# Token-stationary projections behind the first attention input, their transposes, and LayerNorm sums kept in PSUM

## Chip, core and metric

The kernel runs on one core of a Trainium2 chip. The metric is device time of one execution in microseconds. A core has a matrix engine (PE, whose weight loads are a row of their own, PEld), a vector engine (DVE), a scalar engine (ACT), a general engine (POOL) and a queue engine (SP) that issues most transfers. PE writes only to PSUM, which has eight banks of 512 fp32 columns on 128 partitions. Each engine works through its own instructions in program order; semaphores tie the engines to each other and, where the builder asks for it, an engine to its own earlier instructions.

## The reference

Two layers on `x` of 256 tokens by 2048 channels, fp32. Layer one is dilated attention with a gate, layer two a Conformer convolution module with a gate. What matters here:

```python
x = x + mixer_a(rmsnorm(x, g0)) # 3 x 16 heads, ends in  y @ a_w_out   (2048 x 2048)
h = rmsnorm(x, g1)
proj = h @ b_w_in + b_in        # 2048 x 6144
a, ga, z = split(proj, 3)
u = a * sigmoid(ga)
u = causal_depthwise_conv(u, conv_w, width=31) + conv_b
u = (u - mean(u)) * rsqrt(var(u) + EPS) * ln_g + ln_b      # over the 2048 channels
x = x + (silu(u) * silu(z)) @ b_w_out + b_out
```

## The kernel before

Every fp32 product is made of three products of reduced-precision parts: weights `hi` and `lo`, tokens `h` and `l`, in the order hi·h, hi·l, lo·h. Weights come in 480 chunks of 128 x 1024, numbered `n`: 320 for the first input projection (`w_in`), 32 for `w_out`, 96 for the second mixer's input (`v_in`), 32 for `v_out`. The text counts the chunks of `v_in` as k = 0 to 95. `stage(n + 3)` loads chunk n + 3 and has ACT cast `hi`; `low_engine` picks DVE or POOL for `lo` = raw - hi. There are five buffers of each, so a cast for chunk n + 3 needs PE to be done with chunk n - 2.

The main loop runs over n: stage, then the products of chunk n on PE, then the small functions that `at(n, fn)` has put behind that chunk, then `run_line`. Nothing reorders instructions later: what is written first stands first on its engine.

- The first projection (`project`) holds 128 tokens still and moves 512 weight columns: 12 products a chunk.
- All later projections (`project_out`, `products`, `project_b`) hold 128 weight columns still and move 256 tokens: 24 products a chunk, with the result transposed, channels on partitions.
- The convolution is a DVE line (`conv_line`): for each of 16 channel tiles j, `conv_first` has ACT write two accumulators `c[0]` and `c[1]`, `conv_tap` adds 29 taps in turn to one and the other, and `conv_merge` joins them into `d[:, j]`. `run_line` takes from this line as much as its costs (0.4 us a tap) allow per chunk, so the line fills DVE while PE goes through `v_in`. The accumulators lie in two PSUM banks: tags `s` and `o` for even j, two `t` banks for odd j.
- For LayerNorm POOL sums `d` (`usum`, `dsum`) and its squares (`qsum`) in SBUF. After channel 6 a provisional mean `mu` is taken off. `ln_sums` sums over partitions by small products with `ones` on PE, `ln_spread` spreads the scale and the shift over the partitions, and five functions `norm` to `norm_low` per channel pair then make the operands of `v_out`.
- RMS statistics of the second layer (`r1_sums`, `r1_spread`) take a sum over partitions and a spread on PE as well.

Of the kernel before, what the change touches and what calls it, by code (L numbers as in the profile page):

```python
# [17 lines left out]
P = 128  # L18
# [23 lines left out]
def hybrid_kernel(ctx: ExitStack, tc: tile.TileContext, x_perm, x_tok, x_nat, vecs, rel, onehot, maskrow,  # L42
                  w_in, w_out, v_in, v_out, out):
# [31 lines left out]
    units, z_next = [], 0  # L75
    for j in range(KT):
        units += [2 * j, 2 * j + 1]
        if j % 2 and j > 2:
            units.append(32 + z_next)
            z_next += 1  # L80
    units += [32 + j for j in range(z_next, KT)]
# [432 lines left out]

    def project_out(n, n0, mh, ml, tag):

        hi, lo = staged.pop(n)
        m = n - n0
        if m < KT:
            if m == 0:  # L520
                oacc["w"] = [acc_tile(f"{tag}w{i}") for i in range(4)]
            for ct in range(8):
                acc = oacc["w"][ct // 2][:, (ct % 2) * S:(ct % 2 + 1) * S]
                wh, wl = hi[:, ct * P:(ct + 1) * P], lo[:, ct * P:(ct + 1) * P]

                nc.tensor.matmul(acc, lhsT=wh, rhs=mh[:, m, :], start=m == 0 and ct % 2 == 0, stop=False,  # L526
                                 skip_group_check=True)
                nc.tensor.matmul(acc, lhsT=wh, rhs=ml[:, m, :], start=False, stop=False, skip_group_check=True)  # L528
                nc.tensor.matmul(acc, lhsT=wl, rhs=mh[:, m, :], start=False, stop=m == KT - 1, skip_group_check=True)  # L529
                oacc[ct] = acc  # L530
        else:
            ct, half = 8 + (m - KT) // 2, m % 2
            if half == 0:
                oacc[ct] = acc_tile(f"{tag}{ct}")[:, :S]
            products(oacc[ct], hi, lo, half, mh, ml)
# [42 lines left out]
    def h_split(ct):
        g1 = vec[:, V_G1 + ct:V_G1 + ct + 1]
        nc.scalar.activation(f.hh[:, ct, :], f.x1[:, ct, :], AF.Copy, scale=g1)  # L580
        nc.vector.scalar_tensor_tensor(f.hl[:, ct, :], f.x1[:, ct, :], g1, f.hh[:, ct, :].bitcast(F32),
                                       op0=ALU.mult, op1=ALU.subtract)

    at(N_A, load_residual)
    at(N_A + 14, open_second)
    for ct in range(KT):
        if ct < 8:
            at(N_A + KT - 1, residual, ct)
            at(N_A + KT + ct // 2, h_split, ct)
            at(N_A + KT + ct // 2, square_sum, ct)  # L590
        else:
            e = N_A + KT + 2 * (ct - 8) + 1
            at(e, residual, ct)
            at(e, h_split, ct)
            at(e, square_sum, ct)
# [7 lines left out]
    def r1_sums():  # L603
        f.ps = acc_tile("ps_r1")
        token_sums(f.ps, 0, f.ss1)
        st = f.pool.tile([P, 2], F32, name="st_r1")
        nc.vector.tensor_copy(st, f.ps[:, :2])
        f.rc = f.pool.tile([P, 2], F32, name="rc_r1")
        rsqrt_mean(f.rc, st, D, 2)

    def r1_spread():
        spread(f.ps, S, f.rc)
        nc.scalar.copy(f.r1, f.ps[:, S:2 * S])

    at(N_WO, r1_sums)
    at(N_WO + 1, r1_spread)


    acc_b = {}

    def project_b(n):
        hi, lo = staged.pop(n)
        i, half = divmod(n - N_WO, 2)
        if half == 0:
            acc_b[units[i]] = acc_tile(f"b{units[i]}")[:, :S]
        products(acc_b[units[i]], hi, lo, half, f.hh, f.hl)
# [3 lines left out]
    HALF_J = 6  # L630
    clock = [0.0]
# [4 lines left out]
    def run_line(now):  # L636
        clock[0] = max(clock[0], now)
        while line and clock[0] < now + 2.64:
            cost, fn, args = line.pop(0)[1:]
            fn(*args)  # L640
            busy(cost)


    def glu_gate(j):
        f.tg = f.pool.tile([P, S], F32, tag="tg", name=f"tg{j}", bufs=2)
        nc.vector.tensor_tensor(f.tg, acc_b.pop(2 * j + 1), f.r1, op=ALU.mult)
        bg = V_BIN + 16 + j
        nc.scalar.activation(f.tg, f.tg, AF.Sigmoid, bias=vec[:, bg:bg + 1])
        busy(0.34)

    def glu_value(j):
        f.ta = acc_b.pop(2 * j)
        nc.vector.tensor_tensor(f.ta, f.ta, f.r1, op=ALU.mult)
        busy(0.34)

    def glu(j):
        u = f.pool.tile([P, TAPS - 1 + S], F32, tag="u", name=f"u{j}", bufs=3)
        nc.gpsimd.memset(u[:, :TAPS - 1], 0.0)
        nc.vector.scalar_tensor_tensor(u[:, TAPS - 1:], f.ta, vec[:, V_BIN + j:V_BIN + j + 1], f.tg,
                                       op0=ALU.add, op1=ALU.mult)  # L660
        busy(0.4)
        if j == 0:
            conv_line(j, u)
        else:
            at(f.n + 1, conv_line, j, u)
# [25 lines left out]
    def conv_merge(j, c):  # L691
# [6 lines left out]
        if j == 0:  # L698
            nc.gpsimd.tensor_copy(f.usum, f.d[:, 0, :])
        elif j < HALF_J:  # L700
            nc.gpsimd.tensor_tensor(f.usum, f.usum, f.d[:, j, :], op=ALU.add)
            if j == HALF_J - 1:
                at(f.n + 2, mid_sums)
                at(f.n + 4, mid_spread)
        elif j == HALF_J:
# [3 lines left out]
            at(f.n + 1, gather, 0)  # L709
            at(f.n + 2, gather, j)  # L710
            for i in range(1, j):
                at(f.n + 2 + 4 * i, gather, i)
        else:
            gather(j)
            if j == KT - 1:
                at(f.n + 1, ln_sums)

    def mid_sums():

        f.ps = acc_tile("ps_mid")  # L720
        token_sums(f.ps, 0, f.usum)
        f.mc = f.pool.tile([P, 2], F32, name="mc")
        nc.vector.tensor_scalar(f.mc, f.ps[:, :2], 1.0 / (HALF_J * P), None, op0=ALU.mult)

    def mid_spread():
        spread(f.ps, S, f.mc)
        nc.scalar.copy(f.mu, f.ps[:, S:2 * S])

    def gather(j):
        d = f.d[:, j, :]  # L730
        eng = nc.vector if j == KT - 1 else nc.gpsimd
        if j == 0:
            nc.scalar.activation(f.qsum, d, AF.Square)
# [3 lines left out]
        eng.tensor_tensor(f.qsum, f.qsum, sq, op=ALU.add)  # L737

        if j == HALF_J:
            nc.gpsimd.tensor_copy(f.dsum, d)  # L740
        elif j > HALF_J:
            eng.tensor_tensor(f.dsum, f.dsum, d, op=ALU.add)

    def ln_sums():
        f.ps = acc_tile("ps_ln")
        token_sums(f.ps, 0, f.dsum)
        token_sums(f.ps, 2, f.qsum)
# [197 lines left out]
```

## Time and profile before

| what | value |
|---|---|
| median of 3 runs | 1452.47 us (1452.23 to 1452.49) |
| profiled execution, its own time | 1452.36 us |
| its span, first to last instruction | 1450.6 us |
| PE busy | 1442.3 us, 99% |
| DVE busy | 960.2 us, 66% |
| ACT busy | 727.0 us, 50% |
| POOL busy | 423.7 us, 29% |
| `v_in` stage | 1074.1 to 1355.1 us of the span |
| `v_out` stage | 1355.2 to 1447.4 us of the span |
| granted TensorE clock | 1.000 |

The profiled time is 1.8 us over its span and agrees with the median to 0.1 us. Busy time of DVE, ACT and PE counts an instruction from its start to its end; the next one may start before that end, so a pitch (start to start) can be shorter than a duration.

### The profile page before, as it was taken

What the parts mean: (1) busy time and instruction counts of PE and PEld (TensorE: products, weight loads), DVE (VectorE), ACT (ScalarE), POOL (GpSimd) and SP (SyncE); (2) the same over time, 40 slices, a digit from 0 to 9 for tenths busy, and PEclk for the clock granted to TensorE, in tenths of its full rate; (3) what the DMA queues carried; (4) which work ended last, traced back from release to release, by engine and by line L of the source; (5) the groups of instructions that cost most, each with busy time, mean ns of one, the idle gap of its engine ahead of it and who ended that gap; (6) DMA issues with size and microseconds to landing.
All of it is one profiled execution on the core that took longest, in us unless ns stands there. A gap on an engine that the chain in (4) does not pass through costs nothing.

```text
span 1450.6 us, 22407 instructions
## 1 busy us (share of the span) xinstructions
PE 1442.3 (99%) x8524; PEld 1275.6 (88%) x8524; DVE 960.2 (66%) x1542; ACT 727.0 (50%) x1027; POOL 423.7 (29%) x339
## 2 busy tenths in 40 slices
PE   9999999999999999999999999999999999999999
PEld 7778888888888888888888888889999999999999
DVE  6656765765676576576567657646758989997621
ACT  7445554454455455445445545444545545555632
POOL 0210020011011002001001100207217979998544
PEclk9999999999999999999999999999999999999999
DMA  9458556557556655755755665566564655555544
GB/s 360 139 202 251 161 185 206 173 164 217 170 164 197 194 165 181 207 170 170 216 169 164 197 193 165 180 189 218 163 197 165 204 162 182 192 180 184 184 158 142
DMA packets 108699, 271.28 MB, mean 187 GB/s; under 512 B 42416, under 2 KB 44720, under 8 KB 108592
## 3 DMA queue, kind: packets, MB, share of 16 engines
q1 hardware_dynamic: 108160, 269.58, 58.2%
q8 instruction: 67, 1.10, 0.3%
q14 instruction: 40, 0.33, 0.1%
q10 hardware_dynamic: 432, 0.28, 0.1%
HBM read 267.46 MB, written 2.36 MB: 186 GB/s over the span
## 4 chain that ended last, share of the span: by engine, by line
PE 98%; DMA 1%; DVE 0%; ACT 0%; issue 0%; SPq 0%; POOL 0%; POOLq 0%; ACTq 0%
PE acc L290 60%; PE b L541 6%; PE b L542 6%; PE b L543 6%; PE psq L327 1%; PE wow L526 1%; PE vo L543 1%; PE vo L542 1%; PE vo L541 1%; PE vow L529 1%; PE vow L528 1%; PE vow L526 1%; PE wo L543 1%; PE wo L541 1%; PE wo L542 1%; PE wow L528 1%
## 5 line engine op out<-in xcount | busy, mean ns | idle before, releaser
L114 ACT CAST hi<-raw 128x1024 fp32r<-128x1024 f32 x479 | 497.0, 1048 | 292.7 <-PE acc L290 164.2
L117 DVE TENSOR_TENSOR lo<-raw,hi 128x1024 fp32r<-128x1024 f32 x358 | 441.3, 1234 | 282.2 <-ACT hi L114 275.7
L290 PE MATMUL acc<-hi,xh 128*128 128x512 f32 x1280 | 506.0, 397 | 0.1
L290 PE MATMUL acc<-lo,xh 128*128 128x512 f32 x1280 | 497.4, 391 | 0.8 <-DVE lo L117 0.8
L290 PE MATMUL acc<-hi,xl 128*128 128x512 f32 x1280 | 495.9, 389 | 0.0
L117 POOL TENSOR_TENSOR lo<-raw,hi 128x1024 fp32r<-128x1024 f32 x121 | 294.0, 2453 | 120.4 <-ACT hi L114 101.6
L290 PEld LDWEIGHTS acc<-lo,xh 128*128 128x128 f32 x1280 | 240.1, 188 | 53.4 <-DVE lo L117 1.2
L290 PEld LDWEIGHTS acc<-hi,xh 128*128 128x128 f32 x1280 | 240.5, 188 | 49.0 <-issue 2.0
L290 PEld LDWEIGHTS acc<-hi,xl 128*128 128x128 f32 x1280 | 240.8, 188 | 47.1 <-DVE xl L152 0.2
L129 POOL TENSOR_SCALAR rq<-ss 128x4 f32<-128x4 f32 x48 | 10.9, 226 | 789.7 <-DVE ss L309 787.8
L541 PE MATMUL b<-hh,hi 128*128 128x256 f32 x768 | 217.8, 284 | 0.0
L542 PE MATMUL b<-hl,hi 128*128 128x256 f32 x768 | 217.3, 283 | 0.0
L543 PE MATMUL b<-hh,lo 128*128 128x256 f32 x768 | 217.3, 283 | 0.0
L688 DVE SCALAR_TENSOR_TENSOR c<-u,vec,c 128x256 f32<-128x256 f32 x464 | 187.4, 481 | 3.5 <-ACT c L684 3.5
L542 PEld LDWEIGHTS b<-hl,hi 128*128 128x128 f32 x768 | 147.4, 192 | 0.0
L541 PEld LDWEIGHTS b<-hh,hi 128*128 128x128 f32 x768 | 147.4, 192 | 0.0
L543 PEld LDWEIGHTS b<-hh,lo 128*128 128x128 f32 x768 | 147.4, 192 | 0.0
L403 ACT ACTIVATE pr<-sc,m 128x512 f32<-128x512 f32 x32 | 23.1, 723 | 100.8 <-DVE m L401 100.8
L340 DVE TENSOR_TENSOR qk<-psq,qk 128x256 fp32r<-128x256 f32 x48 | 20.3, 422 | 50.6 <-ACT qk L339 50.6
L338 ACT CAST qk<-psq 128x256 fp32r<-128x256 f32 x48 | 17.9, 372 | 64.1 <-PE psq L327 63.6
L130 POOL TENSOR_TENSOR rq<-rq,nhalf 128x4 f32<-128x4 f32 x48 | 48.4, 1008 | 4.0
L422 ACT CAST pp<-pt 128x512 fp32r<-128x512 f32 x32 | 18.8, 587 | 44.1 <-PE pt L414 42.8
(167 smaller groups left out, 1668.0 us busy)
## 6 DMA issues: line engine op xcount, KB each, us to landing
raw<-w_in SPq DMA_DIRECT2D x319, 512.0 KB, 4.2
raw<-v_in SPq DMA_DIRECT2D x96, 512.0 KB, 3.3
raw<-w_out SPq DMA_DIRECT2D x32, 512.0 KB, 4.2
raw<-v_out SPq DMA_DIRECT2D x32, 512.0 KB, 4.1
bt<-btab SPq DMA_DIRECT2D x64, 128.0 KB, 5.8
x_tok<-x_tok SPq DMA_DIRECT2D x4, 512.0 KB, 9.4
x<-x_nat SPq DMA_DIRECT2D x4, 512.0 KB, 6.3
out_t<-ob SPq DMA_DIRECT2D x16, 128.0 KB, 1.8
```

Source lines behind the costliest of these rows:

```text
L114: nc.scalar.copy(hi, raw)
L117: low_engine(n).tensor_tensor(lo, raw, hi.bitcast(F32), op=ALU.subtract)
L130: nc.gpsimd.tensor_tensor(dst, dst, nhalf[:, :n], op=ALU.pow)
L290: nc.tensor.matmul(acc[b], lhsT=(xl if p == 1 else xh)[:, k, sl], rhs=wl if p == 2 else wh, start=k == 0 and p == 0, stop=k == KT - 1 and ...
L340: nc.vector.tensor_tensor(ql, ps[:, 0:2], qh.bitcast(F32), op=ALU.subtract)
L403: nc.scalar.activation(u.pr.rearrange("p a b -> p (a b)"), sc, AF.Exp, bias=u.m[:, 1:2], accum_out=u.m[:, 2:3])
L526: nc.tensor.matmul(acc, lhsT=wh, rhs=mh[:, m, :], start=m == 0 and ct % 2 == 0, stop=False, skip_group_check=True)
L528: nc.tensor.matmul(acc, lhsT=wh, rhs=ml[:, m, :], start=False, stop=False, skip_group_check=True)
L541: nc.tensor.matmul(acc, lhsT=wh, rhs=mh[:, k, :], start=k == 0, stop=False)
L542: nc.tensor.matmul(acc, lhsT=wh, rhs=ml[:, k, :], start=False, stop=False)
L543: nc.tensor.matmul(acc, lhsT=wl, rhs=mh[:, k, :], start=False, stop=k == KT - 1)
L688: nc.vector.scalar_tensor_tensor(c[t % 2], u[:, t:t + S], vec[:, cw + t:cw + t + 1], c[t % 2], op0=ALU.mult, op1=ALU.add)
```

## The change

Behind the first input projection, all projections hold 128 tokens still and move 512 weight columns, as the first one does. The result then has tokens on partitions. So the residual `x1` is kept as tokens by channels, and two sets of PE transposes are new: `x_turn` (eight times four) turns the residual for the second mixer's input, and `turn_group` turns the columns of the second mixer's projection (for each of eight groups with value and gate columns eight transposes, for each of four groups with `z` columns two times four). `take_group` has ACT copy a finished group out of PSUM with the RMS scale, which now is a number per partition; the three DVE scalings and `r1`'s two small steps on PE go. The output bias is loaded once for all partitions (1 MB) and added on DVE in two instructions.

The accumulators use a ring of four banks, and of three while the convolution runs. The fourth bank holds the sums that POOL made before (`f.sums`): DVE and ACT now make them, squares (`squares`) and adds (`gather`). The two accumulators of a channel tile are now the two halves of one bank, `s` or `o`. `CHUNK` is 2.72 us where 2.64 us stood.

```diff
+    def three(acc, xh_, xl_, wh, wl, first, last):
+        nc.tensor.matmul(acc, lhsT=xh_, rhs=wh, start=first, stop=False)
+        nc.tensor.matmul(acc, lhsT=xl_, rhs=wh, start=False, stop=False)
+        nc.tensor.matmul(acc, lhsT=xh_, rhs=wl, start=False, stop=last)
...
-    def products(acc, hi, lo, half, mh, ml):
-        for i in range(8):
-            k = half * 8 + i
-            wh, wl = hi[:, i * P:(i + 1) * P], lo[:, i * P:(i + 1) * P]
-            nc.tensor.matmul(acc, lhsT=wh, rhs=mh[:, k, :], start=k == 0, stop=False)
-            nc.tensor.matmul(acc, lhsT=wh, rhs=ml[:, k, :], start=False, stop=False)
-            nc.tensor.matmul(acc, lhsT=wl, rhs=mh[:, k, :], start=False, stop=k == KT - 1)
...
+    def take_group(g):
+        accs = acc_b.pop(g)
+        ev_b[g] = []
+        for b in range(2):
+            ev = f.pool.tile([P, 512], F32, tag="ev", name=f"ev{g}_{b}", bufs=4)
+            nc.scalar.activation(ev, accs[b], AF.Copy, scale=f.r1[:, b:b + 1])
+            ev_b[g].append(ev)
+    def turn_group(g, part, t):
+        ps = ps_g[g, part] = t_tile(f"pg{g}_{part}", t).rearrange("p (c t) -> p c t", c=2)
+        for c in range(2):
+            for b in range(2):
+                ct = 2 * part + c
+                nc.tensor.transpose(ps[:, c, b * P:(b + 1) * P], ev_b[g][b][:, ct * P:(ct + 1) * P], ident)
...
     def conv_first(j, u, cw, c):
-        tags = (("s", "o"), ("t", "t"))[j % 2]
-        c += [bank(tags[i], f"c{j}_{i}", 2 if tags[i] == "t" else 1)[:, :S] for i in range(2)]
+        ps = bank(("s", "o")[j % 2], f"c{j}", 1)
+        c += [ps[:, :S], ps[:, S:]]
...
-    def gather(j):
+    def squares(j):
...
         sq = f.pool.tile([P, S], F32, tag="sq1", name=f"lsq{j}", bufs=2)
         nc.scalar.activation(sq, d, AF.Square)
-        eng.tensor_tensor(f.qsum, f.qsum, sq, op=ALU.add)
...
+    def gather(j, sq):
+        out_ = f.sb if j == KT - 1 else f.sums
+        if j > HALF_J:
+            nc.vector.tensor_tensor(out_[:, S:], f.sums[:, S:], f.d[:, j, :], op=ALU.add)
+        nc.vector.tensor_tensor(out_[:, :S], f.sums[:, :S], sq, op=ALU.add)
+        if j == KT - 1:
+            ring[:] = [0, 1, 2, 3]
+            at(f.n + 1, ln_sums)
```

How the built program stands at three places. On DVE, where the convolution of channel tile 0 begins (`u0` is its gated input, `c0_0` and `c0_1`, or `c0`, its accumulators; in brackets the semaphores that an instruction waits for; a name like DVE_49 counts the instructions that this engine has finished), before:

```order
L646 TENSOR_TENSOR tg0_9799<-b1_9743,r1_9048 128x256 [waits PE_49]
L117 TENSOR_TENSOR lo359_9804<-raw359_9802,hi359_9803 128x1024 [waits DMAHW0_49,Activation_49]
L659 SCALAR_TENSOR_TENSOR u0_9833<-b0_9671,vec_71,tg0_9799 128x256 [waits DVE_49]
L688 SCALAR_TENSOR_TENSOR c0_0_9836<-u0_9833,vec_71,c0_0_9836 128x256 [waits Activation_49]
L688 SCALAR_TENSOR_TENSOR c0_1_9837<-u0_9833,vec_71,c0_1_9837 128x256 [waits Activation_49]
L688 SCALAR_TENSOR_TENSOR c0_0_9836<-u0_9833,vec_71,c0_0_9836 128x256 [waits DVE_49]
L688 SCALAR_TENSOR_TENSOR c0_1_9837<-u0_9833,vec_71,c0_1_9837 128x256 [waits DVE_49]
```

and after:

```order
L698 SCALAR_TENSOR_TENSOR u0_9262<-pg0_0_9465,vec_71,tg0_9488 128x256 [waits PE_49,Activation_49]
L698 SCALAR_TENSOR_TENSOR u0_9262<-pg0_0_9465,vec_71,tg1_9491 128x256 [waits Activation_49]
L724 SCALAR_TENSOR_TENSOR c0_9512<-u0_9262,vec_71,c0_9512 128x256 [waits DVE_49,Activation_49,Pool_49]
L724 SCALAR_TENSOR_TENSOR c0_9512<-u0_9262,vec_71,c0_9512 128x256 [waits DVE_49] x28
L733 TENSOR_TENSOR d_8866<-c0_9512,half0_9619 128x256 [waits Activation_49]
L724 SCALAR_TENSOR_TENSOR c1_9515<-u0_9262,vec_71,c1_9515 128x256
L724 SCALAR_TENSOR_TENSOR c1_9515<-u0_9262,vec_71,c1_9515 128x256 [waits DVE_49] x16
```

The two accumulators were two tiles; now they are one, and the second tap, which waited for ACT alone, waits for DVE. By the values of these semaphores in the built program, 336 of the 464 taps before waited for the tap two places ahead of them on DVE and none for the instruction just ahead; after, 427 of the 464 wait for the instruction just ahead.

On PE, where a new accumulator of the second mixer begins and the one before is taken out (`b0` and `b1` are units of 128 columns before, `b1_0` and `b1_1` the two token blocks of a group of 512 after, `pg0` the transposed group 0), before:

```order
L542 MATMUL b0_9671<-hl_9044,hi353_9599 128x256
L543 MATMUL b0_9671<-hh_9043,lo353_9600 128x256
L600 MATMUL ps_r1_9696<-ident_72,rc_r1_9701 128x128 x2
L541 MATMUL b1_9743<-hh_9043,hi354_9630 128x256
L542 MATMUL b1_9743<-hl_9044,hi354_9630 128x256
L543 MATMUL b1_9743<-hh_9043,lo354_9631 128x256
```

and after:

```order
L520 MATMUL b1_1_9447<-hi360_9381,hl_8864 128x512
L521 MATMUL b1_1_9447<-lo360_9382,hh_8863 128x512
L672 MATMUL pg0_1_9460<-ident_72,ev0_0_9436 128x128
L672 MATMUL pg0_1_9460<-ident_72,ev0_1_9438 128x128
L672 MATMUL pg0_1_9460<-ident_72,ev0_0_9436 128x128
L672 MATMUL pg0_1_9460<-ident_72,ev0_1_9438 128x128
L672 MATMUL pg0_0_9465<-ident_72,ev0_0_9436 128x128
L672 MATMUL pg0_0_9465<-ident_72,ev0_1_9438 128x128
L672 MATMUL pg0_0_9465<-ident_72,ev0_0_9436 128x128
L672 MATMUL pg0_0_9465<-ident_72,ev0_1_9438 128x128
L519 MATMUL b1_0_9446<-hi361_9399,hh_8863 128x512
```

Eight transposes of group 0 stand behind the first chunk of group 1 (k = 8); at the start of a new accumulator nothing stood before, but for the two products of `r1`'s spread, which are gone.

On PE, where the LayerNorm sums stand (`ps_ln`), before:

```order
L542 MATMUL b44_13163<-hl_9044,hi440_13042 128x256
L543 MATMUL b44_13163<-hh_9043,lo440_13043 128x256
L202 MATMUL ps_ln_13189<-ones_73,dsum_9051 128x1 x2
L202 MATMUL ps_ln_13189<-ones_73,qsum_9052 128x1 x2
L541 MATMUL b44_13163<-hh_9043,hi441_13080 128x256
L542 MATMUL b44_13163<-hl_9044,hi441_13080 128x256
```

and after:

```order
L520 MATMUL b11_1_11723<-hi441_11663,hl_8864 128x512
L521 MATMUL b11_1_11723<-lo441_11664,hh_8863 128x512
L204 MATMUL ps_ln_11772<-ones_73,sb_8869 128x1 x4
L519 MATMUL b11_0_11722<-hi442_11688,hh_8863 128x512
L520 MATMUL b11_0_11722<-hi442_11688,hl_8864 128x512
L521 MATMUL b11_0_11722<-lo442_11689,hh_8863 128x512
```

They stood behind chunk 440 (k = 88) and stand behind chunk 441 (k = 89).

## Rows read from the trace of the kernel before

**Rows 1.** The page: busy time by engine, and the chain's shares by engine.

```profile
PE 1442.3 (99%) x8524; PEld 1275.6 (88%) x8524; DVE 960.2 (66%) x1542; ACT 727.0 (50%) x1027; POOL 423.7 (29%) x339
PE 98%; DMA 1%; DVE 0%; ACT 0%; issue 0%; SPq 0%; POOL 0%; POOLq 0%; ACTq 0%
```

**Rows 2.** Windows: stretch, length, busy us (count) of PE, PEld, DVE, ACT, POOL; clock, DMA.

```profile
1028.10:1074.10 46.00, 46.00 (x385) 46.00 (x385) 32.15 (x41) 24.41 (x42) 11.63 (x14) 1.00 0.52 167
1074.10:1355.10 281.00, 280.32 (x2339) 280.13 (x2338) 240.26 (x583) 149.61 (x216) 237.69 (x138) 1.00 0.56 182
```

**Rows 3.** Timeline of PE, first projection: start, duration, tile (512 columns moving).

```profile
29.70 0.39 PE L290 MATMUL acc<-hi,xh 128*128 128x512 f32 x1
...
36.50 0.39 PE L290 MATMUL acc<-hi,xh 128*128 128x512 f32 x1
```

**Rows 4.** Timeline of PE, second mixer: products with 256 columns moving, sixty apart.

```profile
1325.00 0.28 PE L543 MATMUL b<-hh,lo 128*128 128x256 f32 x1
...
1332.20 0.28 PE L543 MATMUL b<-hh,lo 128*128 128x256 f32 x1
```

**Rows 5.** Chain in order of time, first mixer: start, duration, group, count.

```profile
336.38 0.44 PE psq L327 x4
336.81 2.78 PE acc L290 x12
...
340.03 38.13 PE acc L290 x168
```

**Rows 6.** Chain in order of time, second mixer: the small products and their neighbours.

```profile
1077.30 0.34 PE ps_r L202 x4
...
1080.61 0.45 PE ps_r L600 x4
...
1332.48 0.80 PE ps_ln L202 x8
...
1337.37 0.71 PE ps_rn L600 x4
```

**Rows 7.** Timeline of DVE, first taps of the convolution (merged, with counts).

```profile
1089.93 0.48 DVE L659 SCALAR_TENSOR_TENSOR u<-b,vec,tg 128x256 f32<-128x256 f32 x1
1091.11 5.59 DVE L688 SCALAR_TENSOR_TENSOR c<-u,vec,c 128x256 f32<-128x256 f32 x14 [0.70 <-ACT c L684]
1096.61 0.42 DVE L653 TENSOR_TENSOR b<-b,r 128x256 f32<-128x256 f32 x1
1096.94 4.79 DVE L688 SCALAR_TENSOR_TENSOR c<-u,vec,c 128x256 f32<-128x256 f32 x12
```

**Rows 8.** Timeline of DVE: instructions that use what the one before wrote.

```profile
389.67 0.42 DVE L400 TENSOR_TENSOR sc<-sc,sy 128x256 f32<-128x256 f32 x1
390.13 0.69 DVE L401 TENSOR_REDUCE m<-sc 128x1 f32<-128x512 f32 x1
...
1193.88 0.42 DVE L697 TENSOR_TENSOR d<-c,half 128x256 f32<-128x256 f32 x1
1194.41 2.74 DVE L706 TENSOR_TENSOR d<-d,mu 128x1792 f32<-128x1792 f32 x1
1197.07 1.26 DVE L688 SCALAR_TENSOR_TENSOR c<-u,vec,c 128x256 f32<-128x256 f32 x3
...
1209.82 0.41 DVE L696 TENSOR_TENSOR half<-c,mu 128x256 f32<-128x256 f32 x1
1210.27 0.42 DVE L697 TENSOR_TENSOR d<-c,half 128x256 f32<-128x256 f32 x1
```

**Rows 9.** Groups by line and form: taps, a 512-wide copy from PSUM, sigmoid, cast.

```profile
L114 ACT CAST hi<-raw 128x1024 fp32r<-128x1024 f32 x479 | 497.0, 1048 | 292.7 <-PE acc L290 164.2 <-DMA raw<-w_in 47.3 <-PE vow L528 14.3
L688 DVE SCALAR_TENSOR_TENSOR c<-u,vec,c 128x256 f32<-128x256 f32 x464 | 187.4, 481 | 3.5 <-ACT c L684 3.5
L349 ACT ACTIVATE vh<-acc,r 128x512 fp32r<-128x512 f32 x16 | 10.8, 688 | 8.5 <-PE acc L290 8.5
L648 ACT ACTIVATE tg<-tg,vec 128x256 f32<-128x256 f32 x16 | 8.2, 510 | 31.2 <-DVE tg L646 31.2
```

More of the change, by code (lines that the diff above doesn't have):

```diff
@@ L71, in at @@
         steps.setdefault(n, []).append((fn, args))
[L75 to L81, printed above, removed]
+    NGLU = 8
+    NB = 12
     def source(n):
@@ L520, in project_out @@
             if m == 0:
[L521 to L535, printed above, removed]
@@ L578, in h_split, with residual @@
[L578 to L582, printed above, removed]
+        f.sb = f.pool.tile([P, 512], F32, name="sb")
+    def residual(cg):
+        for b in range(2):
+            xs = f.x1[:, b, cg * 512:(cg + 1) * 512]
+            nc.vector.tensor_tensor(xs, oacc[cg][b], xs, op=ALU.add)
+        oacc.pop(cg)
@@ L603, in r1_sums @@
     def r1_sums():
-        f.ps = acc_tile("ps_r1")
-        token_sums(f.ps, 0, f.ss1)
         st = f.pool.tile([P, 2], F32, name="st_r1")
[L607 to L619, printed above, removed]
+        nc.vector.tensor_reduce(st, f.ss1, op=ALU.add, axis=AX.X)
@@ L621, in project_b @@
+    at(N_WO + 6, bias_add, 1)
+    acc_b, ev_b, ps_g = {}, {}, {}
     def project_b(n):
         hi, lo = staged.pop(n)
[L623 to L626, printed above, removed]
+        g, kc = divmod(n - N_WO, 8)
+        if kc == 0:
+            if g == 0:
+                ring[:] = [i for i in ring if i != 3]
+                open_convolution()
+            acc_b[g] = [acc_tile(f"b{g}_{b}") for b in range(2)]
+        pair(acc_b[g], hi, lo, kc, f.hh, f.hl, kc in (0, 7))
@@ L637, in run_line @@
         clock[0] = max(clock[0], now)
-        while line and clock[0] < now + 2.64:
+        while line and clock[0] < now + CHUNK:
             cost, fn, args = line.pop(0)[1:]
@@ L641, in run_line, with glu @@
             busy(cost)
[L644 to L665, printed above, removed]
+    def glu(g):
+        pa, pg = ps_g.pop((g, 0)), ps_g.pop((g, 1))
+        ev_b.pop(g)
+        for c in range(2):
+            j = 2 * g + c
+            tg = f.pool.tile([P, S], F32, tag="tg", name=f"tg{j}", bufs=2)
+            nc.scalar.activation(tg, pg[:, c], AF.Sigmoid, bias=vec[:, V_BIN + 16 + j:V_BIN + 17 + j])
+            nc.vector.scalar_tensor_tensor(f.u[j][:, TAPS - 1:], pa[:, c], vec[:, V_BIN + j:V_BIN + j + 1], tg,
+                                           op0=ALU.add, op1=ALU.mult)
+            busy(0.4)
+            at(f.n + 1, conv_line, j, f.u[j])
     def conv_line(j, u):
@@ new lines, in hybrid_kernel, with store @@
+    for g in range(NB):
+        e = N_WO + 8 * g + 7
+        at(e, take_group, g)
+        if g < NGLU:
+            at(e + 1, turn_group, g, 1, 1)
+            at(e + 1, turn_group, g, 0, 0)
+            at(e + 2, glu, g)
+        else:
+            for part in range(2):
+                at(e + 1 + 2 * part, turn_group, g, part, 1)
+                at(e + 2 + 2 * part, z_silu, g, part)
+    def store(cg):
+        accs = oacc.pop(cg)
+        for b in range(2):
+            o = f.pool.tile([P, 512], F32, tag="ev", name=f"ob{cg}_{b}", bufs=4)
+            for h in range(1 + (cg == 3 and b == 1)):
+                sl = slice(h * S, (h + 1) * S) if cg == 3 and b == 1 else slice(0, 512)
+                c0 = cg * 512
+                nc.vector.tensor_tensor(o[:, sl], accs[b][:, sl], f.x1[:, b, c0 + sl.start:c0 + sl.stop], op=ALU.add)
+                (nc.sync, nc.scalar)[h].dma_start(out[b * P:(b + 1) * P, c0 + sl.start:c0 + sl.stop], o[:, sl])
```

236 lines of the change are left out of this document (126 added, 110 removed).

## Prediction

> **What bounds the kernel now.** I read the page first: PE is busy 99% of the span and 98% of the chain that ended last is PE, the other engines far behind [rows 1]. Then the windows by stage: PE is busy without a gap through the rest of `w_out`, and for 280.3 of 281.0 us of the second mixer's input projection, while DVE is busy there for 240 us and POOL for 238 [rows 2]. So PE's own pace is the time today, and DVE is the nearest engine behind it, in that one stage. The pace itself comes from timelines of PE. With 512 columns moving, 30 products take 36.50 - 29.70 = 6.80 us, 226.7 ns each [rows 3]; with 256 columns, 60 products take 7.20 us, 120.0 ns each [rows 4]. A chunk of weights thus costs 12 x 226.7 = 2.72 us in the first form and 24 x 120.0 = 2.88 us in the second.
>
> **Part 1, wider products.** 160 chunks (32 + 96 + 32) go from 2.88 to 2.72 us: -25.6 us of PE work. The instruction is the one that the first projection uses, with the same operands' order.
>
> **Part 2, transposes.** Four transposes stand 0.44 us in the chain, and the chunk behind them takes 2.78 us, where 14 undisturbed chunks take 38.13 us, 2.72 each [rows 5]: 0.50 us for four, 0.94 for eight. The change adds eight fours for the residual (4.0), eight eights (7.5) and eight fours for `z` (4.0): +15.5 us of PE work.
>
> **Part 3, small things on PE.** The sum and spread for `r1` go: 0.34 + 0.45 us and a break of about 0.1 at each [rows 6], -1.0. The LayerNorm sums and their spread stay, with the same chain behind them (from the end of the sums, 1333.3, to the spread, 1337.4: 4.1 us [rows 6], one chunk of it covered then as now). At the start of `v_out` the four-bank ring gives the first accumulator the bank of the last token block of group 11, which ACT copies out only when PE is done with it; the nearest copy of 512 columns takes 0.69 us [rows 9], and with the handovers I take +0.85, where before a free bank stood there. Elsewhere a reused bank has half a chunk or more (1.36 us) for its copy. The last stores end on one more add, +0.35 from the pitch of an add, 1096.94 - 1096.61 [rows 7]. The bias load (1 MB) and its two adds on DVE fall where DVE has only `lo` to make and casts are up to three chunks (8 us) ahead: nothing; if that cover failed, at most the two adds, 3 us each by the 2.74 us for 1792 columns [rows 8].
>
> PE alone would so end at 1452.4 - 25.6 + 15.5 - 1.0 + 0.85 + 0.35 = 1442.5 us.
>
> **Part 4, the taps.** Today 14 taps take 1096.61 - 1091.11 = 5.50 us, a pitch of 0.393 us [rows 7], though one lasts 0.481 [rows 9]: the next begins 0.09 before the end, which it can, since it works on the other accumulator. The change puts both accumulators into one tile, and the order of the built program shows what becomes of the waits: 427 of 464 taps now wait until the tap just ahead of them has ended. No tap before shows such a wait, so its price is bounded by other pairs that have it. The sum of two halves follows its operand 0.45 us later, which is that operand's 0.41 and a gap of 0.04; the reduction follows its sum 0.46 later, again a gap of 0.04; the subtraction of the mean has the widest gap, 0.11 (1193.88 + 0.42 to 1194.41) [rows 8]. The lower bound is a tap that starts as the other ends, 0.48; the upper 0.59. I take 0.52, by the nearest form, 256 columns on one bank's data; that is +0.128 us a tap.
>
> The VectorE page of the Trainium skill (VectorE: DVE Perf Modes, section "The DRAIN you can't avoid") says otherwise: eight copies took 13.88 us with a semaphore after each and also with one after the last alone, so a wait would cost nothing extra. By it a tap would stay at 0.393 us and the time would be that of the first rival below. The pairs in rows 8 against the pitch in rows 7 don't agree with it.
>
> DVE's work from the first tap to the last LayerNorm add, by starts:
> - 427 x 0.52 + 37 x 0.39 = 236.5 us of taps
> - 16 ends of a channel, a halved sum and an add, 0.45 + 0.35 [rows 8] = 12.8 (for the first seven ACT makes the half; I take the same)
> - five running sums that wait for the instruction ahead, 0.45 each = 2.3
> - the mean's subtraction, 1197.07 - 1193.88 less the add = 2.9 [rows 8]
> - LayerNorm adds, six at 0.33, nine pairs at 0.45 + 0.33 = 9.0, new on DVE
> - 14 gated products, 0.42 each by the pitch of taps and adds = 5.9
> - the wait for the last square on ACT, about 0.9
>
> Together 270.3 us. Off DVE go POOL's former work and three scalings, both not in this list. The first tap can start about 29 us into the stage: nine chunks 24.5, two fours 1.0, the first four of the next transposes 0.4, sigmoid 0.51 and a cast 1.05 on ACT [rows 9], and from the product to the first tap 1.2 [rows 7], with handovers. So DVE is done at 299.3 us.
>
> PE comes to the LayerNorm sums, behind k = 89, after 90 x 2.72 + 1.0 + 8 x 0.94 + 5 x 0.50 + 0.9 (provisional mean) = 256.7 us of its own work. It would then wait 42.6 us, most of it earlier and in pieces: ACT's queue holds the copies of halves and the squares ahead of the casts of later chunks, so ACT waits for DVE with weights behind it, and PE runs out of them. Where PE stands does not matter for the sum; nothing of `v_out` can start without the norm.
>
> Of part 1, the 90 chunks before that point are then covered by DVE. **Sum: 1442.5 + 42.6 = 1485.1 us**, against 1452.36 in the profiled execution, which is 0.1 from the median.
>
> **Rivals.**
> - *The waits cost nothing* (taps at 0.393 us). DVE is done at 299.3 - 427 x 0.128 = 244.6 us, before PE. Then PE is the bound; only the seven squares in a row behind the mean's subtraction hold up ACT's casts, by an estimated 10 us (2.7 of subtraction, seven squares and adds in turn at about 0.7, and the casts' own wait), where three chunks, 8 us, are covered: about +1.5. That gives 1444, faster. It decides at the tap's pitch: DVE's margin is 12 us and PE's gain 10, 22 us over 427 taps, so below 0.44 us a tap the change wins. For it speaks that today's busy DVE is already hidden; against it, every pair in rows 8.
> - *The clock falls while PE waits.* The granted clock is 1.00 in all stages [rows 2], but PE hardly ever waits. If a part f of the 257 us ran at the lower level, 1.2 GHz, PE needs 257 x (1 + f); that counts beyond f = 0.17, and f = 0.35 would give +48, about 1533.
> - *Wide products with tokens of the second layer don't reach 226.7 ns* but stay at 240 for 512 columns. Only the 79 or so chunks outside the covered stretch would pay, 79 x 0.16 = 12.6: 1498. Against it: same form, same tiles' layout as rows 3.
>
> **How the numbers follow.** Forecast 0.86, waits free 0.08, clock 0.03, slow products 0.03. The forecast's own ends are the pair bounds: 0.48 a tap takes off 427 x 0.04 = 17 us, 1468; 0.59 adds 30, 1515. A first tap or a copy misjudged by a few us moves it by as much. I say 1466 to 1512: the free waits lie below, the clock above. Chances, with 0.2% (3 us) as what a measurement tells from no change: faster 0.09, within 0.01, slower 0.90.
>
> **What would show it.** Taps follow each other at 0.52 us; the last LayerNorm add ends near 299 us into the stage, at about 1371 us of the span; PE is idle some 43 us in that stage, waiting for casts that wait for DVE, and for the sums; `v_out` begins near 1391 and lasts 88 us; in undisturbed stretches 12 products take 2.72 us and four transposes 0.5. The forecast is wrong if taps keep a pitch near 0.39, or if PE's gaps have another releaser than DVE's line.

## Result and profile after

The change makes the kernel slower: 1500.97 us (median of four runs, 1497.83 to 1501.77) against 1452.48 us, a ratio of 1.033 with a 95% interval of 1.0317 to 1.0342. The forecast was 1485.1 within 1466 to 1512; the sign and the mechanism hold, the size falls 16 us short.

The page of the changed kernel, its profiled execution (1497.83 us): busy time by engine and the chain's shares.

```profile
PE 1448.0 (97%) x6724; PEld 1192.5 (80%) x6724; DVE 1005.7 (67%) x1511; ACT 732.7 (49%) x1037; POOL 380.6 (25%) x278
PE 79%; DVE 16%; ACT 2%; issue 1%; DMA 1%; POOL 0%; SPq 0%; DVEq 0%; ACTq 0%
```

In [rows 1] the chain was PE for 98%. Now 16% of it is DVE, and 12 of these 16 are taps. The windows of the three last stages (columns as in [rows 2]: length, busy us of PE, PEld, DVE, ACT, POOL, then clock):

```profile
1074.30:1379.00 304.70, 270.64 (x1182) 218.84 (x1180) 271.76 (x552) 139.34 (x204) 190.77 (x84) 0.96 0.51 154
1379.00:1402.30 23.30, 20.74 (x92) 16.87 (x92) 14.68 (x19) 13.76 (x23) 11.53 (x7) 0.93 0.38 119
1402.30:1491.60 89.30, 88.72 (x391) 72.47 (x392) 37.27 (x38) 38.95 (x49) 50.23 (x20) 1.00 0.51 169
```

From the start of the `v_in` stage to the LayerNorm sums, DVE is busy 271.8 of 304.7 us (and its first tap starts 30 us into the stage), while PE idles 34 us; in [rows 2] PE idled 0.7 us. Timeline of DVE, the first channel's taps and the last channel's end (start, duration, count; merged groups run from the first start to the last end):

```profile
1104.14 15.19 DVE L724 SCALAR_TENSOR_TENSOR c<-u,vec,c 128x256 f32<-128x256 f32 x29 [1.46 <-ACT c L721]
1119.77 0.42 DVE L733 TENSOR_TENSOR d<-c,half 128x256 f32<-128x256 f32 x1 [0.44 <-ACT half L730]
...
1378.61 0.42 DVE L780 TENSOR_TENSOR sb<-sums,d 128x256 f32<-128x256 f32 x1
1379.06 0.42 DVE L781 TENSOR_TENSOR sb<-sums,lsq 128x256 f32<-128x256 f32 x1
```

The pitch is (15.19 - 0.489) / 28 = 0.525 us, where it was 0.393 [rows 7]; one tap lasts 0.489 us, little more than before [rows 9]. Each tap now begins 0.04 us behind the end of the one ahead; before it began 0.09 ahead of that end. What PE waited for in these stages (waiter, releaser, us in total, times, longest), and what ACT waited for:

```profile
PE b L519 <- ACT ev L663: 10.0, 3, 5.5
PE b L521 <- POOL lo L119: 8.6, 5, 1.7
PE sums L204 <- ACT sb L740: 6.4, 1, 6.4
PE b L519 <- ACT hi L116: 4.0, 5, 1.2
PE ps_ln L204 <- DVE sb L780: 3.3, 1, 3.3
```

```profile
ACT lsq L768 <- DVE d L733: 66.2, 9, 11.8
ACT half L730 <- DVE c L724: 52.8, 7, 10.3
```

PE's releasers are ACT and POOL, but ACT itself stands at a channel's half or square until DVE has done the taps, with casts (`hi`) and block copies (`ev`) behind it in its queue, and POOL makes `lo` from `hi`. Read alone, the first list would blame ACT, which is busy 139 of 305 us.

The stages of four kernels and of the forecast in us, each from its first product to the next stage's first. "Forecast" is the prediction's terms put into their stages (its 0.85 for the start of `v_out` stands in `v_in`, whose row ends with the first product of `v_out`); the two on the right are experiments told of below.

| stage | before | forecast | after | four taps less, in turn | best version |
|---|---|---|---|---|---|
| up to `w_out` | 973.6 | 973.6 | 974.5 | 975.6 | 973.6 |
| `w_out` | 100.7 | 98.6 | 99.9 | 99.8 | 99.8 |
| `v_in` | 280.9 | 277.9 + 42.6 | 327.9 | 282.7 | 276.5 |
| `v_out`, first to last product | 92.0 | 87.0 | 89.3 | 89.5 | 90.7 |
| last product to the end | 3.4 | 3.7 | 4.3 | 4.4 | 4.4 |
| span | 1450.6 | 1483.4 | 1496.0 | 1451.9 | 1445.0 |

### The profile page after: what moved, and what is told of

It reads as the page before. It is cut to its first block, busy times and chain, and to the rows that moved or that the text cites. A ratio compares the mean times of both kernels' runs of the same rounds, so it can differ in the third digit from the quotient of the medians.

```text
span 1496.0 us, 18614 instructions
## 1 busy us (share of the span) xinstructions
PE 1448.0 (97%) x6724; PEld 1192.5 (80%) x6724; DVE 1005.7 (67%) x1511; ACT 732.7 (49%) x1037; POOL 380.6 (25%) x278
## 4 chain that ended last, share of the span: by engine, by line
PE 79%; DVE 16%; ACT 2%; issue 1%; DMA 1%; POOL 0%; SPq 0%; DVEq 0%; ACTq 0%
PE acc L292 58%; DVE c L724 12%; PE vo L521 2%; PE vo L519 2%; PE vo L520 2%; PE wo L519 2%; PE wo L521 2%; PE wo L520 2%; PE b L519 1%; PE psq L329 1%; PE b L520 1%; PE b L521 1%; PE pt L416 1%; ACT hi L116 1%; PE s L385 1%
## 5 line engine op out<-in xcount | busy, mean ns | idle before, releaser
L724 DVE SCALAR_TENSOR_TENSOR c<-u,vec,c 128x256 f32<-128x256 f32 x464 | 227.0, 489 | 16.4 <-ACT c L721 1.5
L519 PE MATMUL b<-hi,hh 128*128 128x512 f32 x384 | 156.2, 407 | 14.0 <-ACT ev L663 10.0
L521 PE MATMUL b<-lo,hh 128*128 128x512 f32 x384 | 153.7, 400 | 8.6 <-POOL lo L119 8.6
L520 PE MATMUL b<-hi,hl 128*128 128x512 f32 x384 | 153.2, 399 | 0.0
L519 PEld LDWEIGHTS b<-hi,hh 128*128 128x128 f32 x384 | 74.7, 194 | 32.2 <-ACT ev L663 11.6
L521 PEld LDWEIGHTS b<-lo,hh 128*128 128x128 f32 x384 | 74.2, 193 | 27.1 <-POOL lo L119 11.1
L520 PEld LDWEIGHTS b<-hi,hl 128*128 128x128 f32 x384 | 74.5, 194 | 14.8
L519 PE MATMUL vo<-hi,bh 128*128 128x512 f32 x128 | 50.2, 392 | 1.9 <-ACT ev L663 1.9
L519 PE MATMUL wo<-hi,yh 128*128 128x512 f32 x128 | 51.4, 401 | 0.0
L521 PE MATMUL vo<-lo,bh 128*128 128x512 f32 x128 | 50.2, 392 | 0.5 <-POOL lo L119 0.5
```

The costliest lines, as they stand in the source:

```text
L519: nc.tensor.matmul(acc, lhsT=xh_, rhs=wh, start=first, stop=False)
L520: nc.tensor.matmul(acc, lhsT=xl_, rhs=wh, start=False, stop=False)
L521: nc.tensor.matmul(acc, lhsT=xh_, rhs=wl, start=False, stop=last)
L724: nc.vector.scalar_tensor_tensor(c[t % 2], u[:, t:t + S], vec[:, cw + t:cw + t + 1], c[t % 2], op0=ALU.mult, op1=ALU.add)
```

## Experiments

The theory: the wait for the tap just ahead costs 0.13 us a tap and makes DVE's line the bound. Rivals: the same slow line for another reason (memory, more work on DVE), PE's clock, wide products that are slower than their rows.

**The one part alone.** The kernel before, with both accumulators in one bank:

```diff
-        tags = (("s", "o"), ("t", "t"))[j % 2]
-        c += [bank(tags[i], f"c{j}_{i}", 2 if tags[i] == "t" else 1)[:, :S] for i in range(2)]
+        ps = bank(("s", "o")[j % 2], f"c{j}", 1)
+        c += [ps[:, :S], ps[:, S:]]
```

> The kernel before with that one part alone: both accumulators of a channel are halves of one PSUM bank, all else as it was. Theory: taps at 0.52 us, some 400 of them that wait, 51 us more for DVE, which before had 41 us of the stage idle but starts its taps 16 us into it; by the list of its work DVE would end some 25 us behind the place where the LayerNorm sums stand today: 1470 to 1485. Rival (DVE's idle time hides it): within 3 us of 1452.5.

Measured 1489.00 us against 1451.92, ratio 1.0257 (1.0242 to 1.0272): this part alone costs 37 us, a little more than expected. Its DVE timeline:

```profile
1091.76 7.32 DVE L688 SCALAR_TENSOR_TENSOR c<-u,vec,c 128x256 f32<-128x256 f32 x14 [1.26 <-ACT c L685]
```

The pitch is (7.32 - 0.49) / 13 = 0.525 us, with nothing else changed. From this first tap to the LayerNorm sums (1367.3) are 275.5 us; in the changed kernel, from 1104.14 to 1379.09, they are 275.0. The lines are equally long, and the changed kernel's starts 12.4 us later, since a group of eight chunks must be done before its first channel. That is how the rest of the change, which should bring 10 us on PE, ends up losing another 12.

**DVE's line as the bound.** The changed kernel without the last two taps of each channel:

```diff
     def conv_tap(u, cw, c, t):
+        if t >= TAPS - 2:
+            return
```

> The changed kernel without the last two taps of every channel (this part of the convolution is left out; the order of all other instructions is as it was). Theory (DVE's line sets the time from the first tap to the LayerNorm sums): 32 taps x 0.525 = 16.8 us less, 1483 to 1485.5. Rival (PE at a lower clock, or ACT's casts, set it): the time falls by less than 5 us.

Measured 1482.80 us, 18.2 less than the changed kernel, just beyond the expected end; 16.8 are the taps, the other 1.4 are not explained. Time off DVE's line comes off the whole, so PE, ACT and the clock don't set the end there.

**The wait taken away by another memory.** The second accumulator as a tile of SBUF:

```diff
-        c += [ps[:, :S], ps[:, S:]]
+        c += [ps[:, :S], f.pool.tile([P, S], F32, tag="c1", name=f"c1_{j}", bufs=2)]
```

> The changed kernel with one thing undone: a channel's second accumulator is a tile of SBUF instead of the other half of the first one's bank, so that a tap waits for the tap two ahead, not for the one just ahead. Theory (the wait for the tap just ahead is the whole loss): the pitch of the taps goes from 0.525 back to about 0.39 us, DVE's line is shorter by 427 x 0.13 = 57 us and ends before PE comes to the LayerNorm sums; PE is the bound again and the time is 1444 to 1448, below the kernel before. Rival (DVE's line is long for other reasons, or two operands on one memory cost the time): the pitch stays above 0.48 and the time stays within 5 us of 1501.

Measured 1575.24 us, ratio 1.0852: outside both expectations. Taps of this kernel (least, median and longest duration in ns), and two windows of its first channel (columns as above):

```profile
L724 DVE SCALAR_TENSOR_TENSOR c<-u,vec,c x464: 464/476/2649, 1104.9 to 1455.5; 128x256 f32<-128x256 f32 x155
```

```profile
1104.90:1117.20 12.30, 12.30 (x56) 10.20 (x55) 12.26 (x10) 5.36 (x7) 11.98 (x5) 1.00 0.60 209
1117.30:1125.00 7.70, 5.39 (x24) 4.13 (x22) 7.67 (x20) 0.40 (x1) 0.00 (x0) 1.00 0.19 70
```

With POOL idle, 20 taps take 7.70 us, 0.385 each: the wait is gone and the pitch of before is back, which is what the theory says. With POOL busy 11.98 of 12.30 us, only ten taps fit. Half of the taps now read both operands from SBUF, and such a tap takes up to 2.65 us, the length of one `lo` on POOL (2.4 to 2.6 us). The Trainium skill (SBUF — State Buffer, sections "SBUF: two separate sides" and "Who interferes with whom") states this: a vector instruction with two SBUF inputs and a GpSimd instruction that reads SBUF exclude each other for the whole instruction. The two windows agree with it. The changed kernel, with one operand in PSUM, ran 25 instructions on DVE beside the same work of POOL:

```profile
1104.10:1117.20 13.10, 13.10 (x60) 10.84 (x59) 12.22 (x25) 5.05 (x6) 10.95 (x5) 1.00 0.66 200
```

**The wait taken away by order** (`taps_in_turn`)**.** The changed kernel's banks, taps and work, with the first twelve taps of a channel put one by one between the last twelve of the channel ahead, which has the other bank:

```diff
-        for t in range(2, TAPS):
-            line.append((("tap", j), 0.4, conv_tap, (u, cw, c, t)))
+        mine = [(("tap", j), 0.4, conv_tap, (u, cw, c, t)) for t in range(2, TAPS)]
+        others = [i for i, x in enumerate(line) if x[0] == ("tap", j - 1)][-MIX:]
+        first_of_mine, mine = mine[:len(others)], mine[len(others):]
+        for i, x in reversed(list(zip(others, first_of_mine))):
+            line.insert(i + 1, x)
+        line.extend(mine)
```

> The changed kernel with the same banks, the same taps and the same work, only in another order: twelve of the first taps of a channel go between the last twelve taps of the channel ahead of it, one by one. The two channels have their accumulators in different banks, so that most taps wait for the tap two ahead. Theory (the wait for the tap just ahead is the loss; memory and work are not): taps in turn have a pitch of 0.39 us, those left alone 0.52; of a channel's 29 taps some 22 are in turn, so DVE's line is shorter by about 16 x 22 x 0.13 = 46 us and ends at about 1333, where PE comes to the LayerNorm sums; 1444 to 1458. Rival (the accumulators' place, two halves of a bank, makes a tap slow whatever stands ahead of it): taps stay at 0.52 us in any order and the time stays within 5 us of 1501.

Measured 1456.48 us (1455.50 to 1458.20), ratio to before 1.0031 (1.0020 to 1.0042), 44.5 us less than the changed kernel, by order alone. Its DVE timeline:

```profile
1104.21 18.42 DVE L729 SCALAR_TENSOR_TENSOR c<-u,vec,c 128x256 f32<-128x256 f32 x41 [1.46 <-ACT c L726]
...
1274.06 11.06 DVE L729 SCALAR_TENSOR_TENSOR c<-u,vec,c 128x256 f32<-128x256 f32 x27
...
1337.70 0.42 DVE L786 TENSOR_TENSOR sb<-sums,lsq 128x256 f32<-128x256 f32 x1
```

The 27 taps, most of them in turn, have a pitch of (11.06 - 0.48) / 26 = 0.407 us; DVE's line ends 41 us earlier. Place and work are the changed kernel's, so the rival "a tap on half a bank is slow whatever stands ahead" falls, and the cause of the loss is settled: the wait for the tap just ahead. But the time is not 1444, and it is not below the kernel before.

**What PE alone gives.** The same with four taps of each channel left out, so that DVE is early (edit as above, with `TAPS - 4`):

> taps_in_turn without the last four taps of every channel (this part of the convolution is left out), so that DVE is done well before PE needs the sums: 64 taps x 0.42 = 27 us off DVE's line, which then ends near 1311, against PE's arrival at about 1331. It asks what PE alone gives for the change: by the prediction's parts 1 to 3 1442.5, plus 2.3 us by which the stage began later than forecast, some 1445; 1443 to 1448 confirms the sum of parts 1 to 3. A time above 1451 would mean that wide products and transposes bring less than their rows say, or that another wait holds PE.

Measured 1452.96 us (1452.05 to 1455.79): above 1451, so parts 1 to 3 of the prediction bring less than their sum. DVE was early by less than expected: its last add starts at 1333.05, not near 1311, but PE comes to the sums only at 1336.8 and does not wait for it. What PE waited for behind the first projection:

```profile
PE b L519 <- ACT ev L663: 3.1, 1, 3.1
PE vo L519 <- ACT ev L663: 1.9, 1, 1.9
PE vo L521 <- POOL lo L119: 0.7, 2, 0.4
PE pt L416 <- DVE pp L425: 0.5, 1, 0.5
PE ps_rn L613 <- DVE rn L804: 0.3, 1, 0.3
```

The longest has its origin in ACT's queue, in the timeline of ACT:

```profile
1209.47 0.39 ACT L772 ACTIVATE sums<-d 128x256 f32<-128x256 f32 x1 [6.62 <-DVE d L751]
...
1213.13 0.42 ACT L775 ACTIVATE lsq<-d 128x256 f32<-128x256 f32 x1 [0.30 <-DVE sums L788]
1213.46 1.03 ACT L116 CAST hi<-raw 128x1024 fp32r<-128x1024 f32 x1
...
1216.34 1.26 ACT L663 ACTIVATE ev<-b,r 128x512 f32<-128x512 f32 x2
```

ACT stands 6.6 us for the subtraction of the mean, then makes seven squares in step with DVE's adds; the casts and the block's copies come behind them, and PE has no free accumulator for 3.1 us. The same wait is in the kernel with taps in turn (3.12 us).

**Three smaller edits.** The first: `taps_in_turn` with the banks of `v_out` in another order:

```diff
+                if tag == "vo":
+                    ring[:] = [i for i in range(4) if i not in taken[-2:]] + taken[-2:]
+                    turns["acc"] = 3
```

> taps_in_turn, and the last projection's first accumulators take the banks that are free longest, the banks of the last group of the projection ahead only for its third and fourth. Where PE stood 1.9 us at the start of the last projection until ACT had copied the last group out, it should now stand 0.3 at most: 1 to 1.6 us below taps_in_turn. If something else ends that wait (the norm's casts), the two are equal.

Measured 1457.57 us, no gain. In the trace of `taps_in_turn` the wait for the copy is 0.8 us, not the 1.9 that the expectation starts from (the changed kernel's). Here it is gone from the list, and waits for POOL's `lo` have grown from 0.9 to 2.1 us; that the earlier start of `v_out` makes POOL late is likely, but not shown. The second: the changed kernel with 16 useless products ahead of the LayerNorm sums:

```diff
         f.ps = t_tile("ps_ln", 0)
+        for i in range(16):
+            nc.tensor.matmul(f.ps, lhsT=f.hh[:, i, :P], rhs=f.hh[:, 0:2, :], start=True, stop=True)
```

> The changed kernel with 16 products of 512 columns of no use ahead of the LayerNorm sums, 3.6 us at full clock, where PE idles 3.3 us for the last add and runs its next 8 products at the lower level. If the fall of the clock there is a price of that idle time, these 8 products run at full clock again and the time falls by about 1.6 us, to 1499; DVE's line and so the start of the sums stay where they are. If the lower clock has its cause in the longer waits ahead, nothing changes, or the time rises by what the 16 products stand in the way, up to 1 us.

Measured 1500.32 us (1498.75 to 1501.51), within the scatter. The clock did what was expected (12 products behind the sums in 2.86 us instead of 4.43). In that execution DVE's last add came 2 us later, at 1381.02 instead of 1379.06, so the times can't be compared, but the stretch from there to the second half of the LayerNorm's spread can. Timeline of PE, the changed kernel first:

```profile
1386.10 0.71 PE L613 MATMUL ps_rn<-ident,rn 128*128 128x128 f32 x4 [0.61 <-DVE rn L797]
```

```profile
1388.07 0.71 PE L613 MATMUL ps_rn<-ident,rn 128*128 128x128 f32 x4 [1.61 <-DVE rn L799]
```

It is 7.04 us with the fall of the clock and 7.05 with the useless products and without it: what PE gains it then waits for DVE's `rn`. This fall of the clock cost nothing. The third: `taps_in_turn` with the LayerNorm's running sums back on POOL and in SBUF:

```diff
-            nc.vector.tensor_tensor(f.sums[:, S:], f.sums[:, S:], f.d[:, j, :], op=ALU.add)
+            nc.gpsimd.tensor_tensor(f.usum, f.usum, f.d[:, j, :], op=ALU.add)
...
-            for i in (0, j, *range(1, j)):
-                squares(i)
+            at(f.n + 1, gather, 0)
+            at(f.n + 2, gather, j)
+            for i in range(1, j):
+                at(f.n + 2 + 4 * i, gather, i)
```

> taps_in_turn with the running sums of the LayerNorm on POOL and in SBUF again, as in the kernel before (the last channel's on DVE); the squares are gathered one by one, four chunks apart, as before. DVE loses some 5 x 0.45 + 18 x 0.4 + 8 x 0.35 = 12 us, its line ends near 1325 and PE gets to the sums first: 1445 to 1450, below the kernel before by 2 to 7 us. If POOL's queue (lo and sums) becomes late instead, PE waits for lo in this stage and the time stays at 1456 or above.

Measured 1454.12 us (1452.17 to 1456.16), 2.4 less than `taps_in_turn`, less than expected. The 3.1 us wait is gone (0.3 left). PE's timeline shows what came in its place:

```profile
1321.04 0.39 PE L521 MATMUL b<-lo,hh 128*128 128x512 f32 x1
1324.13 1.01 PE L204 MATMUL ps_ln<-ones,dsum 128*128 128x1 f32 x4 [2.71 <-DVE dsum L784]
1325.00 0.99 PE L204 MATMUL ps_ln<-ones,qsum 128*128 128x1 f32 x4
1325.86 0.77 PE L519 MATMUL b<-hi,hh 128*128 128x512 f32 x1
1326.43 0.63 PE L520 MATMUL b<-hi,hl 128*128 128x512 f32 x1
```

PE idles 2.7 us for the last sums, and the next 11 products start 0.43 us apart instead of 0.227: the granted clock there is 0.51 (1326.4 to 1330.9), the lower of its two levels, 1.2 instead of 2.4 GHz.

**Toward a better version.** On top of the third edit, the LayerNorm sums two chunks later in PE's order, then their spread one chunk later too:

```diff
-                at(f.n + 1, ln_sums)
+                at(f.n + 3, ln_sums)
...
-        at(f.n + 1, ln_spread)
+        at(f.n + 2, ln_spread)
```

> in_turn_pool_sums with the LayerNorm sums two chunks later in PE's order. There PE came to them 2.7 us ahead of DVE's last add and ran its next 11 products at the lower clock, 0.43 us instead of 0.227, another 2.3 us, and the sums themselves slower. Two chunks are 5.4 us: DVE is done first, PE doesn't idle and its clock doesn't fall there; 2.7 + 2.3 to 3 us less, 1448 to 1450, below the kernel before. If the norm, now 5.4 us later, ends too late for the last projection's first products, PE idles at its start instead and nothing is gained.

With the first edit alone 1453.14 us, not the 1448 to 1450 expected and not below the kernel before; the runs spread from 1450.26 to 1455.05, and they go with the granted clock: 1450.26, 1450.28 and 1450.84 at 0.999 to 1.000, 1455.00 and 1455.05 at 0.996. From the first product of `v_in` to the first of `v_out` PE gained 2.4 us (281.6 to 279.2) of the 5 expected, since it now waits 1.5 and 1.6 us at the spread, for POOL's and DVE's small steps.

> in_turn_pool_sums_late with the LayerNorm's spread one chunk later (where PE stood 1.5 and 1.6 us for POOL's and DVE's small steps of the norm) and, in the last projection, every second low part on DVE instead of every third (where PE stood 1.8 us for POOL). If these waits are what is left of the idle time, and the falls of the clock behind them, 4 to 5 us go and the runs lie closer together: 1447 to 1450, below the kernel before. If the norm's delay reaches the start of the last projection, it is 1452 to 1455 as now.

With both edits, and every second `lo` of `v_out` on DVE instead of every third, 1456.18 us, above both expectations: `v_in` fell to 276.5 us, `v_out` grew from 90.5 to 99.1.

> in_turn_spread_late with the last projection's low parts as they were (every third on DVE). The spread one chunk later took 2.7 us out of the projection ahead (276.5 instead of 279.2 from its first product to the first of the last projection); the last projection itself grew from 90.5 to 99.1 us. If the low parts moved to DVE did that (DVE's queue of norm steps ahead of them), it is back at 90.5 and the time is 1450 to 1451, 0.1% below the kernel before; if the later norm did it, it stays at 1454 to 1457.

With both edits and the `lo` of `v_out` as they were, **1447.45 us** (1446.77 to 1449.74), ratio to before 0.9974 (0.9964 to 0.9984): 2.5 us below the least that was expected, 0.3% below the kernel before, and below the changed one. So it was the `lo` moved to DVE that made `v_out` longer, not the later spread. Its windows of `v_in` and `v_out`:

```profile
1073.40:1349.90 276.50, 275.54 (x1274) 228.74 (x1273) 246.55 (x543) 152.83 (x220) 224.62 (x120) 1.00 0.57 180
1349.90:1440.80 90.90, 88.84 (x393) 72.42 (x391) 36.36 (x38) 39.67 (x50) 51.40 (x20) 1.00 0.51 167
```

PE is busy again for 275.5 of 276.5 us, and its clock stays up.

## Why the prediction was right, and where it was not

**Part 4, the wait.** Right in mechanism and nearly in size. Pitch 0.52 forecast, 0.525 measured; 427 x 0.005 = 2.1 us. (The upper pair bound, 0.59, gives 1515, beyond the prediction's own 1512.) The Trainium skill (VectorE: DVE Perf Modes, section "The DRAIN you can't avoid") would have it cost nothing; the measured pitches, 0.525 with the wait and 0.385 to 0.407 without, don't agree, for taps of this form.

**Part 4, the list of DVE's work.** 270.3 us forecast, 275.3 measured (1104.14 to 1379.48): the pitch's 2.1, two waits for a sigmoid, 1.75 together, which the list didn't have, and about 1 in small gaps. The first tap came 29.7 us into the stage, 29.0 forecast. With the stage itself late, the last add ended at 1379.5, not at 1371.

**PE's idle time.** 43 us forecast; 34.8 us of waits up to the spread, while the stage was 51 us longer than PE's own 277. Most of the rest is the lower clock, 0.96 over 304.7 us, some 12 us. So the second rival was no alternative, it came along: behind each of the four waits of 3.3 to 6.4 us stood products at the lower level, and behind some shorter ones too (1.7 and 1.95 us, but not behind others of 1.7). While DVE sets the end this costs nothing, since the rival's break-even (0.17 of the stage) isn't reached. Timeline of PE at the LayerNorm sums:

```profile
1375.41 0.39 PE L521 MATMUL b<-lo,hh 128*128 128x512 f32 x1
1379.09 1.05 PE L204 MATMUL ps_ln<-ones,sb 128*128 128x1 f32 x8 [3.30 <-DVE sb L780]
1380.01 0.76 PE L519 MATMUL b<-hi,hh 128*128 128x512 f32 x1
1380.57 0.63 PE L520 MATMUL b<-hi,hl 128*128 128x512 f32 x1
1380.99 0.63 PE L521 MATMUL b<-lo,hh 128*128 128x512 f32 x1
```

The twelve products of that chunk take 4.43 us instead of 2.86, but as the 16 useless products show, the time doesn't rise by it: the spread waits for DVE. The median of the runs, 3.1 us above the profiled one, goes with a clock of 0.986 to 0.988 against 0.991; where these 3.1 us lie, no trace shows.

**Parts 1 to 3, "PE alone would so end at 1442.5".** This step failed: with DVE early, PE gives some 1453. By the table the products and transposes in `v_in` are right: 277.0 forecast (without the 0.85), 276.5 in the version whose PE hardly waits there; twelve products take 2.72 us and four transposes about 0.45. What was mis-sized lies around them, and in the kernel with four taps less, whose profiled execution is 11.2 us above 1442.5, it adds up to 10.7 us:
- up to `w_out`: 2.0 us in that run, 0.9 in the changed kernel, none in the best version. This is no steady cost of the change, and its cause stays open; in that run the granted clock was 0.99 over the first 200 us.
- `w_out`: 99.8 instead of 98.6, among it a wait of 0.5 us of PE's attention transposes for DVE's `pp`.
- `v_in`: the squares behind the mean's subtraction, 3.1 us. The prediction had them in its first rival alone, at 1.5.
- the start of `v_out`: 2.1 us behind the last product of `v_in`, 0.85 forecast; ACT makes two copies (1.27 us together) behind a cast of 1.04.
- `v_out`: 89.5 instead of 87.0, with 0.7 of waits for POOL's `lo`; last stores 1.0 instead of 0.35.

In the changed kernel the pieces are 2.3 us before `v_in`, 0.7 to the first tap, 5.0 in DVE's line, 1.7 from the last add to `v_out`, 2.3 in `v_out` and 0.6 at the end: 12.6 us, against 12.7 between forecast and profiled execution. Some 7 of them belong to parts 1 to 3, 5.7 to part 4. The 1.7 have a cause that part 3 set at nothing, "the same chain": from the end of the LayerNorm sums to the spread it took 4.1 us before and takes 6.0 now (1380.1 to 1386.1), because DVE's small steps stand behind a `lo` on POOL twice instead of once (last section). The misses all point the same way; that the time still lies within the range is due to its width, which was set for the tap and not for these terms.

**The rivals.** "The waits cost nothing: 1444" was too good: with the waits nearly gone, the change stands at 1456.5, and with DVE relieved as well at 1453.0. Its break-even, a pitch of 0.44, was therefore wrong: with taps in turn the average is some 0.43 (0.525 less 41 us over 427 taps), and the change still loses 0.3%. "Wide products stay slow" falls: 0.227 us in all stages. The bias adds (2.29 us each, done before the first tap) are not among what PE or DVE waited for, as forecast.

## What to carry to other kernels

Where an engine runs a long chain of short instructions, look at what each waits for in the built program: two chains in turn on separate banks let one instruction start before the other ends, and joining their tiles to save a bank can cost a quarter of the chain's pace (0.525 against 0.393 us). If the banks are needed, change the order, not the memory: two neighbouring channels in turn gave back 44.5 us with the same banks. A sum over PE's instructions is a lower bound: of the 10 us that it promised, 5 are missing even in the best version, 2.1 of them waits for POOL's `lo` in `v_out`; look also at the copies, casts and small steps that a new layout puts into the other engines' queues.

## What was not expected of the hardware

That DVE waits out a whole instruction of POOL when its operands both lie in SBUF, as seen with the second accumulator in SBUF, holds for tiny instructions too. DVE's statistics of the LayerNorm (2 columns), before first:

```profile
1333.50 0.16 DVE L751 TENSOR_TENSOR vv<-st_ln 128x2 f32<-128x2 f32 x1
...
1334.98 2.34 DVE L755 SCALAR_TENSOR_TENSOR rn<-st_ln,rn 128x2 f32<-128x2 f32 x1 [1.12 <-POOL rn L130]
```

```profile
1380.38 2.06 DVE L793 TENSOR_TENSOR vv<-st_ln 128x2 f32<-128x2 f32 x1
1382.47 0.16 DVE L794 TENSOR_TENSOR vv<-st_ln,vv 128x2 f32<-128x2 f32 x1
1383.73 2.31 DVE L797 SCALAR_TENSOR_TENSOR rn<-st_ln,rn 128x2 f32<-128x2 f32 x1 [1.10 <-POOL rn L132]
```

And POOL, before and after:

```profile
1334.92 5.80 POOL L117 TENSOR_TENSOR lo<-raw,hi 128x1024 fp32r<-128x1024 f32 x2
```

```profile
1380.04 2.38 POOL L119 TENSOR_TENSOR lo<-raw,hi 128x1024 fp32r<-128x1024 f32 x1 [4.97 <-ACT hi L116]
...
1383.67 2.36 POOL L119 TENSOR_TENSOR lo<-raw,hi 128x1024 fp32r<-128x1024 f32 x1
```

The subtraction `vv` takes 0.16 us before and 2.06 after, where a `lo` has begun on POOL just ahead of it, and ends with that `lo`; `rn`, as small, has a `lo` just ahead of it in both and takes 2.3. That is twice in the changed kernel's chain to `v_out`, once in that of before.

The granted clock can fall behind short waits: 2.7 us of idle PE were followed by 11 products at the lower level (2.3 us of PE's time), and 3.3 us by eight; with the 3.3 us filled by products it did not fall there. Runs of one kernel that differ by 5 us, as 1450.3 and 1455.0, have a clock of 1.000 and 0.996; of the slower ones no trace is kept, so it is open whether the clock is the cause or follows from longer waits. What sets how often it falls in a run stays open.
